# A streaming batch-norm: loads and stores on two DMA rings with hand-placed semaphores, and the last tile handled as two halves of its rows

## The chip, the cores and the metric

The kernel runs on one core of one Trainium2 chip. Times are device microseconds (us); "before" and "after" are medians of several executions on the same chip. All runs quoted here are of the state "fast" (no run was set aside), with a granted clock of 1.0. A profile shows one execution of each kernel; its span is about 1.8 us shorter than the time of that execution.

## The reference

An inference batch-norm over a tensor of 32 x 256 x 128 x 128 float32 values. For each channel there is one scale and one shift:

```python
def reference(x, gamma, beta, running_mean, running_var):
    eps = 1e-5
    # the four vectors of 256 channels are reshaped to (1, 256, 1, 1)
    return gamma * (x - mean) / np.sqrt(var + eps) + beta
```

It reads 536.9 MB and writes as much; there is one multiply-add per element. The kernel sees `x` as 64 tiles of 128 channels (partitions) by 16384 columns, 8 MB each, so that one partition's row of a tile is 64 KB.

## The kernel before

Three buffers, one DMA ring (a queue of transfers; every load and store of a tile is issued by SyncE, SP in the profile), in groups of three tiles: three loads, then three stores, then the next three loads.

```python
NBUF = 3
GROUPS = [3] * 20 + [2, 2]
AHEAD = 0
# ... parameters: scale_t, shift_t, one column per half of the channels ...

    def load(i):
        t = data.tile([P, HW], f32, tag="t")          # P = 128, HW = 16384
        nc.sync.dma_start(out=t[:], in_=xr[i])
        tiles[i] = t

    def compute(i):
        t = tiles[i]
        cb = i % NCB
        nc.vector.tensor_scalar(out=t[:], in0=t[:],
            scalar1=scale_t[:, cb : cb + 1], scalar2=shift_t[:, cb : cb + 1],
            op0=mybir.AluOpType.mult, op1=mybir.AluOpType.add)

    def store(i):
        t = tiles.pop(i)
        nc.sync.dma_start(out=outr[i], in_=t[:])

    first = 0
    for g, size in enumerate(GROUPS):
        idxs = range(first, first + size)
        for i in idxs:
            compute(i)
        for i in idxs:
            store(i)
        first += size
        # ... load the tiles of the next group ...
```

## Time and profile before

| | |
|---|---|
| time, median | 2486.68 us (2486.56 to 2487.64, 3 runs) |
| DMA engines busy | 99.9% of the span |
| VectorE (DVE) busy | 566.0 us, 23% |
| 64 KB packets | 16384, minimum and median 2.418 us |

First the page of the kernel before: busy time of VectorE; the mean GB/s in 40 equal slices of the span; and the one DMA queue that carries the tiles, with its packets, its MB and the share of 16 engines' span that the packets took.

```profile
DVE 566.0 (23%) x75; ACT 1.6 (0%) x2; POOL 0.2 (0%) x4
GB/s 421 423 439 439 425 436 439 431 431 439 431 431 439 435 426 436 436 431 435 435 435 427 439 434 427 439 434 427 439 437 432 432 437 433 431 437 433 431 437 396
q1 hardware_dynamic: 18432, 1073.75, 99.9%
```

The DMA engines are the bound, from the first slice to the last. The trace's packet records give the unit: one 64 KB row, loaded or stored, takes one DMA engine 2.418 us. Each of 16 engines has 1024 of them, 2476.0 us. The span is 2483.6 us, so only 7.6 us are anything else.

Then the groups of instructions: the 64 passes of VectorE. The columns after the count are busy us, mean ns of one, and idle us before them with what ended most of it.

```profile
L93 DVE TENSOR_SCALAR t<-t,scale_t,shift_t 128x16384 f32<-128x16384 f32 x64 | 564.0, 8812 | 1863.9 <-DMA t<-in_x_dram 1863.8
```

A pass takes 8.81 us, and VectorE idles 1863.9 us waiting for loads. That idle time costs nothing here: the DMA engines are busy for 99.9% of the span meanwhile.

Last, the end of the run in the timeline: start, duration, engine, instruction, and in brackets the idle time before it.

```profile
2424.58 8.81 DVE L93 TENSOR_SCALAR t<-t,scale_t,shift_t 128x16384 f32<-128x16384 f32 x1 [49.09 <-DMA t<-in_x_dram]
2433.42 19.69 SPq L104 DMA_DIRECT2D out_dram<-t  x2
2443.92 8.81 DVE L93 TENSOR_SCALAR t<-t,scale_t,shift_t 128x16384 f32<-128x16384 f32 x1 [10.53 <-DMA t<-in_x_dram]
```

Tile 62 lands at 2424.58 and tile 63 at 2443.92, each starting its pass at once. While the last pass runs to 2452.7, the store of tile 62, issued at 2433.42, has the engines. The last store follows it. The engines are not left without work anywhere in this tail, as windows of 10 us show: length, busy us of each engine with its count of instructions, TensorE's clock, the DMA engines' busy share, and GB/s. (A packet is counted by its start, so that the share of a full window lies somewhat under or over 1.)

```profile
2443.60:2453.60 10.00, 8.81 (x1) 0.00 (x0) 0.00 (x0) 1.00 0.98 426
2453.60:2463.60 10.00, 0.00 (x0) 0.00 (x0) 0.00 (x0) 1.00 1.07 465
2463.60:2473.60 10.00, 0.00 (x0) 0.00 (x0) 0.00 (x0) 1.00 0.97 419
```

A store is about 19.3 us of work for all engines (8 packets of 2.418 us each).

### The profile page before, as it was taken

How to read it: one execution, taken by the hardware profiler on the slowest of the kernel's cores; microseconds unless marked ns; L12 is line 12 of the kernel's file. 1: busy time of each engine (PE TensorE's matmuls, PEld its weight loads, DVE VectorE, ACT ScalarE, POOL GpSimd, SP SyncE). 2: the span in 40 equal slices, each digit the busy share in tenths (PEclk: the TensorE clock that was granted, in tenths of full speed). 3: DMA queues.
4: the chain of work that ended last, by engine and by line, in shares of the span. 5: the costliest groups of instructions: out<-in, count | busy, mean ns of one | idle time of the engine just before them, and what ended most of it. 6: DMA issues, size and time to landing. Idle time of an engine off the chain costs nothing.

```text
span 2483.6 us, 383 instructions
## 1 busy us (share of the span) xinstructions
DVE 566.0 (23%) x75; ACT 1.6 (0%) x2; POOL 0.2 (0%) x4
## 2 busy tenths in 40 slices
DVE  3140404121221213140403121221213040403112
ACT  0000000000000000000000000000000000000000
POOL 0000000000000000000000000000000000000000
DMA  9999999999999999999999999999999999999999
GB/s 421 423 439 439 425 436 439 431 431 439 431 431 439 435 426 436 436 431 435 435 435 427 439 434 427 439 434 427 439 437 432 432 437 433 431 437 433 431 437 396
DMA packets 18442, 1073.77 MB, mean 432 GB/s; under 512 B 2052, under 2 KB 2056, under 8 KB 2056
## 3 DMA queue, kind: packets, MB, share of 16 engines
q1 hardware_dynamic: 18432, 1073.75, 99.9%
q14 instruction: 2, 0.02, 0.0%
q10 hardware_dynamic: 8, 0.00, 0.0%
HBM read 536.88 MB, written 536.87 MB: 432 GB/s over the span
## 4 chain that ended last, share of the span: by engine, by line
another core or an unknown queue 72%; DVE 22%; DMA 4%; issue 0%; DVEq 0%; SPq 0%
DVE t L93 22%; DMA t<-in_x_dram 4%; DVEq L93 0%; SPq L51 0%; SPq L104 0%
## 5 line engine op out<-in xcount | busy, mean ns | idle before, releaser
L93 DVE TENSOR_SCALAR t<-t,scale_t,shift_t 128x16384 f32<-128x16384 f32 x64 | 564.0, 8812 | 1863.9 <-DMA t<-in_x_dram 1863.8
L66 DVE STREAM_TRANSPOSE turned<-rows 32x256 f32<-32x256 f32 x1 | 0.4, 432 | 21.5 <-DMA rows<-in_running_mean_dram 21.5
L78 ACT ACT_TABLE_LOAD x1 | 1.3, 1283 | 2.6 <-issue 2.6
L71 DVE COPY par<-turned 32x8 f32<-32x8 f32 x4 | 0.6, 161 | 0.1
L56 DVE MEMSET rows<- 32x256 f32 x1 | 0.3, 272 | 0.8 <-PEq L132 0.8
L78 ACT ACTIVATE tmp_t<-par,eps_t 128x2 f32<-128x2 f32 x1 | 0.3, 297 | 20.0 <-DVE par L71 20.0
L85 DVE RECIPROCAL tmp_t<-tmp_t 128x2 f32<-128x2 f32 x1 | 0.2, 165 | 0.4 <-ACT tmp_t L78 0.4
L87 DVE TENSOR_TENSOR tmp_t<-par,scale_t 128x2 f32<-128x2 f32 x1 | 0.2, 161 | 0.0
L88 DVE TENSOR_TENSOR shift_t<-par,tmp_t 128x2 f32<-128x2 f32 x1 | 0.2, 161 | 0.0
L86 DVE TENSOR_TENSOR scale_t<-par,tmp_t 128x2 f32<-128x2 f32 x1 | 0.2, 160 | 0.0
L132 POOL MEMSET const-uint8-127<- 128x1 uint8 x1 | 0.1, 103 | 0.0
L132 POOL MEMSET const-bfloat16-1.0<- 128x1 bf16 x1 | 0.1, 101 | 0.0
L132 POOL MEMSET const-float32-0.0<- 128x1 f32 x1 | 0.1, 98 | 0.2 <-issue 0.2
L132 POOL MEMSET const-float32-1.0<- 128x1 f32 x1 | 0.1, 98 | 0.0
L64 DVE MEMSET eps_t<- 128x1 f32 x1 | 0.1, 59 | 0.0
## 6 DMA issues: line engine op xcount, KB each, us to landing
t<-in_x_dram SPq DMA_DIRECT2D x64, 58.0
out_dram<-t SPq DMA_DIRECT2D x64, 49.1
rows<-in_running_var_dram ACTq DMA_DIRECT2D x1, 1.0 KB
rows<-in_gamma_dram ACTq DMA_DIRECT2D x1, 1.0 KB
rows<-in_beta_dram ACTq DMA_DIRECT2D x1, 1.0 KB
rows<-in_running_mean_dram ACTq DMA_DIRECT2D x1, 1.0 KB
```

The lines of the kernel that those rows point to most:

```text
L56: nc.vector.memset(rows, 0.0)
L64: nc.vector.memset(eps_t, eps)
L66: nc.vector.transpose(out=turned[:], in_=rows[:])
L71: nc.vector.tensor_copy(out=par[q * B : (q + 1) * B], in_=blocks[:, :, q, 0:4])
L78: nc.scalar.activation(out=tmp_t[:], in_=var_t, func=mybir.ActivationFunctionType.Sqrt, bias=eps_t[:], scale=1.0,)
L85: nc.vector.reciprocal(out=tmp_t[:], in_=tmp_t[:])
L86: nc.vector.tensor_mul(out=scale_t[:], in0=gamma_t, in1=tmp_t[:])
L87: nc.vector.tensor_mul(out=tmp_t[:], in0=mean_t, in1=scale_t[:])
L88: nc.vector.tensor_sub(out=shift_t[:], in0=beta_t, in1=tmp_t[:])
L93: nc.vector.tensor_scalar(out=t[:], in0=t[:], scalar1=scale_t[:, cb : cb + 1], scalar2=shift_t[:, cb : cb + 1], op0=mybir.AluOpType.mult, ...
L132: nc = _bacc.Bacc("TRN2", target_bir_lowering=False, num_devices=1)
```

## The change

Its intent: loads on the SP ring and stores on the ring of ScalarE (ACT), so that neither waits behind the other; semaphores (counters on which one engine waits for another) placed by hand instead of by the scheduler; and the last tile cut into partitions 0 to 63 and 64 to 127, so that the first half can be stored while the second is still being loaded or computed. The diff's core (the parameter arithmetic is the same, with waits spelled out):

```diff
 NBUF = 3
-GROUPS = [3] * 20 + [2, 2]
 ...
+        last = NT - 1
+        half = [slice(0, P // 2), slice(P // 2, P)]
+        for i in range(NT):
+            s, turn = i % NBUF, i // NBUF
+            if i < last:
+                inst = nc.sync.dma_start(out=bufs[s][:], in_=xr[i]).then_inc(loaded[s], 16)
+                if turn:
+                    inst._wait_ge(stored[s], 16 * turn)
+            else:
+                for h in range(2):
+                    inst = nc.sync.dma_start(out=bufs[s][half[h]], in_=xr[i][half[h]]).then_inc(halves[h], 16)
+                    if h == 0:
+                        inst._wait_ge(stored[s], 16 * turn)
 ...
+        def compute(i, rows=slice(0, P)):       # as before, on bufs[s][rows]; then_inc(done, 1)
+        def store(i, rows=slice(0, P)):
+            s = i % NBUF
+            return nc.scalar.dma_start(out=outr[i][rows], in_=bufs[s][rows]).then_inc(stored[s], 16)
+
+        for i in range(last):
+            compute(i)._wait_ge(loaded[i % NBUF], 16 * (i // NBUF + 1))
+            store(i)._wait_ge(done, i + 1)
+        for h in range(2):
+            compute(last, half[h])._wait_ge(halves[h], 16)
+            store(last, half[h])._wait_ge(done, last + h + 1)
+        for s in range(NBUF):
+            turns = (NT - s + NBUF - 1) // NBUF
+            nc.sync.wait_ge(stored[s], 16 * (turns + (1 if last % NBUF == s else 0)))
```

More of the change, by code (lines that the diff above doesn't have):

```diff
@@ L9 @@
 NBUF = 3
-GROUPS = [3] * 20 + [2, 2]
-AHEAD = 0
 @with_exitstack
@@ L37 @@
     NQ = P // B
-    assert sum(GROUPS) == NT and max(GROUPS) <= NBUF
-    params = ctx.enter_context(tc.tile_pool(name="params", bufs=1))
-    data = ctx.enter_context(tc.tile_pool(name="data", bufs=NBUF))
     xr = x.rearrange("n (cb p) h w -> (n cb) p (h w)", p=P)
     outr = out.rearrange("n (cb p) h w -> (n cb) p (h w)", p=P)
-    ctx.enter_context(tc.manual_schedule())
-    tiles = {}
-    def load(i):
-        t = data.tile([P, HW], f32, tag="t")
-        nc.sync.dma_start(out=t[:], in_=xr[i])
-        tiles[i] = t
@@ L55 @@
-    rows = params.tile([B, C], f32, tag="rows")
-    nc.vector.memset(rows, 0.0)
-    for r, ap in enumerate((running_var, gamma, beta, running_mean)):
-        nc.scalar.dma_start(out=rows[r : r + 1, :], in_=ap.rearrange("(o c) -> o c", o=1))
-    for i in range(AHEAD + GROUPS[0]):
-        load(i)
-    eps_t = params.tile([P, 1], f32, tag="eps")
-    nc.vector.memset(eps_t, eps)
-    turned = params.tile([B, C], f32, tag="turned")
-    nc.vector.transpose(out=turned[:], in_=rows[:])
-    par = params.tile([P, NCB, 4], f32, tag="par")
@@ L69 @@
-    blocks = turned.rearrange("p (cb q r) -> p cb q r", cb=NCB, q=NQ)
-    for q in range(NQ):
-        nc.vector.tensor_copy(out=par[q * B : (q + 1) * B], in_=blocks[:, :, q, 0:4])
-    var_t, gamma_t, beta_t, mean_t = (par[:, :, r] for r in range(4))
-    scale_t = params.tile([P, NCB], f32, tag="scale")
-    shift_t = params.tile([P, NCB], f32, tag="shift")
-    tmp_t = params.tile([P, NCB], f32, tag="tmp")
-    nc.scalar.activation(
-        out=tmp_t[:],
-        in_=var_t,
-        func=mybir.ActivationFunctionType.Sqrt,
-        bias=eps_t[:],
-        scale=1.0,
-    )
@@ L85 @@
-    nc.vector.reciprocal(out=tmp_t[:], in_=tmp_t[:])
-    nc.vector.tensor_mul(out=scale_t[:], in0=gamma_t, in1=tmp_t[:])
-    nc.vector.tensor_mul(out=tmp_t[:], in0=mean_t, in1=scale_t[:])
-    nc.vector.tensor_sub(out=shift_t[:], in0=beta_t, in1=tmp_t[:])
-    def compute(i):
-        t = tiles[i]
-        cb = i % NCB
-        nc.vector.tensor_scalar(
-            out=t[:],
-            in0=t[:],
-            scalar1=scale_t[:, cb : cb + 1],
-            scalar2=shift_t[:, cb : cb + 1],
-            op0=mybir.AluOpType.mult,
-            op1=mybir.AluOpType.add,
-        )
@@ L102, in store @@
-    def store(i):
-        t = tiles.pop(i)
-        nc.sync.dma_start(out=outr[i], in_=t[:])
-    first = 0
-    for g, size in enumerate(GROUPS):
-        idxs = range(first, first + size)
-        for i in idxs:
-            compute(i)
-        for i in idxs:
-            store(i)
-        first += size
-        more = GROUPS[g + 1] if g + 1 < len(GROUPS) else 0
-        for i in range(first + AHEAD, min(first + AHEAD + more, NT)):
-            load(i)
+    params = ctx.enter_context(tc.tile_pool(name="params", bufs=1))
@@ new lines @@
+    data = ctx.enter_context(tc.tile_pool(name="data", bufs=1))
+    bufs = [data.tile([P, HW], f32, name=f"t{s}", tag=f"t{s}") for s in range(NBUF)]
+    rows = params.tile([B, C], f32, name="rows", tag="rows")
+    turned = params.tile([B, C], f32, name="turned", tag="turned")
+    par = params.tile([P, NCB, 4], f32, name="par", tag="par")
+    eps_t = params.tile([P, 1], f32, name="eps_t", tag="eps")
+    std_t = params.tile([P, NCB], f32, name="std_t", tag="std")
+    rstd_t = params.tile([P, NCB], f32, name="rstd_t", tag="rstd")
@@ new lines @@
+    scale_t = params.tile([P, NCB], f32, name="scale_t", tag="scale")
+    ms_t = params.tile([P, NCB], f32, name="ms_t", tag="ms")
+    shift_t = params.tile([P, NCB], f32, name="shift_t", tag="shift")
+    loaded = [tc.alloc_semaphore(f"loaded{s}") for s in range(NBUF)]
+    stored = [tc.alloc_semaphore(f"stored{s}") for s in range(NBUF)]
+    done = tc.alloc_semaphore("done")
+    fetched = tc.alloc_semaphore("fetched")
+    vec = tc.alloc_semaphore("vec")
+    act = tc.alloc_semaphore("act")
@@ new lines, with step @@
+    halves = [tc.alloc_semaphore(f"half{h}") for h in range(2)]
+    with tc.tile_critical():
+        count = [0]
+        def step(inst, sem=None, value=None):
+            if sem is not None:
+                inst._wait_ge(sem, value)
+            elif count[0]:
+                inst._wait_ge(vec, count[0])
+            inst.then_inc(vec, 1)
+            count[0] += 1
+            return count[0]
+        last = NT - 1
[11 more added lines that the diff above has]
+                        inst._wait_ge(stored[s], 16 * turn)
+        step(nc.vector.memset(eps_t[:], eps))
+        zeroed = step(nc.vector.memset(rows[:], 0.0))
+        for r, ap in enumerate((running_var, gamma, beta, running_mean)):
+            inst = nc.scalar.dma_start(out=rows[r : r + 1, :], in_=ap.rearrange("(o c) -> o c", o=1))
+            if r == 0:
+                inst._wait_ge(vec, zeroed)
+            inst.then_inc(fetched, 16)
+        step(nc.vector.transpose(out=turned[:], in_=rows[:]), fetched, 64)
+        blocks = turned.rearrange("p (cb q r) -> p cb q r", cb=NCB, q=NQ)
+        for q in range(NQ):
+            placed = step(nc.vector.tensor_copy(out=par[q * B : (q + 1) * B], in_=blocks[:, :, q, 0:4]))
+        var_t, gamma_t, beta_t, mean_t = (par[:, :, r] for r in range(4))
+        nc.scalar.activation(
+            out=std_t[:],
+            in_=var_t,
+            func=mybir.ActivationFunctionType.Sqrt,
+            bias=eps_t[:],
+            scale=1.0,
+        )._wait_ge(vec, placed).then_inc(act, 1)
+        step(nc.vector.reciprocal(out=rstd_t[:], in_=std_t[:]), act, 1)
+        step(nc.vector.tensor_mul(out=scale_t[:], in0=gamma_t, in1=rstd_t[:]))
+        step(nc.vector.tensor_mul(out=ms_t[:], in0=mean_t, in1=scale_t[:]))
+        ready = step(nc.vector.tensor_sub(out=shift_t[:], in0=beta_t, in1=ms_t[:]))
+        nc.vector.wait_ge(vec, ready)
+        def compute(i, rows=slice(0, P)):
+            s, cb = i % NBUF, i % NCB
+            return nc.vector.tensor_scalar(
+                out=bufs[s][rows],
+                in0=bufs[s][rows],
+                scalar1=scale_t[rows, cb : cb + 1],
+                scalar2=shift_t[rows, cb : cb + 1],
+                op0=mybir.AluOpType.mult,
+                op1=mybir.AluOpType.add,
+            ).then_inc(done, 1)
+        def store(i, rows=slice(0, P)):
[10 more added lines that the diff above has]
+            nc.sync.wait_ge(stored[s], 16 * (turns + (1 if last % NBUF == s else 0)))
```

## The prediction

> What bounds the kernel. The page's DMA rows show the 16 DMA engines busy 99.9% of the span of 2483.6 us on one queue, moving 1073.77 MB at 432 GB/s. The trace's packet records hold 16384 packets of 64 KB whose minimum and median are both 2.418 us, for loads and stores alike, so 1024 packets per engine need 2476.0 us. VectorE is busy 23%; its 64 passes of 8.81 us hide behind transfers. The timeline of the end shows no bubble: the last load lands at 2443.9, the store of the tile before fills the last pass (to 2452.8), and the last store then takes its 19.4 us. Room for a gain: the 7.6 us between 2476.0 and 2483.6 (0.3%), unless the packet time changes.
>
> What the change does.
> (a) Loads stay on the SP ring, stores move to the ACT ring. [...] four 1 KB parameter loads on the ACT ring landed at 22.6 us, their 8 packets one per 2.42 us, that is in turn with the 64 KB packets of the other ring. With three buffers a cycle is 116 us (period in the chain of waits); a load and a store at half rate each (about 38.7 us) plus a pass of 8.8 us need 86 us, so neither ring runs dry.
> (b) Loads and stores now alternate packet by packet instead of. In the old trace only the packets at a turn from load to store are slow: about 0.1 us per engine at a typical turn, 1.2 us at the first. If every alternation paid this, 512 turns would cost 50 us; I expect 0 to 15 us.
> (c) The last tile is halved by partitions. Passes of half the partitions still take 8.8 us each (16384 columns), hidden. [...] No transfer of 64 partitions is in the trace. If it holds, the last loads (8 packets per engine, at 4.84 instead of 2.42 us) cost up to 19 us more, partly hidden by interleaved stores, and the last two stores 19 us more with nothing to hide them. If it does not hold, halving wins nothing, since the old tail has no bubble. I give the penalty two chances in three.
> (d) Hand-placed semaphores remove waits of the SP queue that are off the bound: under 3 us.
>
> Sum: 2486.7 + about 5 (mixing) + about 17 (halves, weighted; 30 when it applies) - 2 gives about 2506 us. Range 2480 to 2532. Faster by over 2%: 0.03; within 2%: 0.88; slower by over 2%: 0.09.
>
> What would show it. DMA busy near 99%; the 64 KB packets of the steady part still 2.42 us; a store landing every 38.7 us. (c) right: the last 64-partition transfers have packets near 4.8 us, GB/s in the last two slices falls well below 396, and the end comes some 50 us after the last load instead of 40. (c) wrong: those packets stay at 2.42 us and the time is 2482 to 2490.
>
> What would make it wrong: read-write mixing that costs 5% in every packet (slower by more than 2%), or mixing that lets an engine's load and store overlap so that packets of both rings take less than 2.42 us in effect (faster). Either shows in the GB/s row.

(In (c), "it" and "the penalty" mean a supposition, shown by no trace at that time: that a transfer of 64 partitions takes twice the 2.42 us per packet, hence 4.84. Measured since: medians of 4.5 to 5.0 us per packet in the changed kernel and 5.11 us in E6, with 17.8 us of excess for the halved load alone (E5) and 20.2 us for the halved store alone (E6), where (c) has up to 19 and 19. The sum: 2486.7 + 5 + 17 - 2 = 2506.7.)

## The result, and the profile after

2524.93 us median of 4 runs (2520.78 to 2531.57) against 2486.62 us for the kernel before on the same chip: a ratio of 1.0156, 95% interval 1.0133 to 1.0179. So the change costs 38 us, within 2% but clear of noise. Ratios here are the mean time of one kernel's fast runs over that of the other's runs of the same rounds, so not quite the ratio of the medians quoted.

The page after: the GB/s row and the two queues.

```profile
GB/s 415 431 431 433 440 436 432 432 432 432 433 436 438 433 429 432 431 432 433 435 433 425 431 432 432 432 432 432 432 432 432 432 432 432 432 432 432 432 342 256
q1 hardware_dynamic: 9232, 536.88, 50.2%
q10 hardware_dynamic: 9240, 536.88, 49.6%
```

The 38 slices before the last two look like before; the last two fall from 437 and 396 GB/s to 342 and 256. The loads now go through q1 and the stores through q10, half the time each.

The passes by shape:

```profile
L119 DVE TENSOR_SCALAR t<-t,scale_t,shift_t 128x16384 f32<-128x16384 f32 x63 | 555.2, 8813 | 1860.9 <-DMA t<-in_x_dram 1860.7
L119 DVE TENSOR_SCALAR t<-t,scale_t,shift_t 64x16384 f32<-64x16384 f32 x2 | 17.6, 8810 | 35.2 <-DMA t<-in_x_dram 35.2
```

Half the partitions take as long as all of them, 8.81 us; half the columns take 4.55 us (E3 below). So the columns set the time of these passes.

The end in the timeline (the last load's halves are issued from 2421.34 on):

```profile
2421.34 5.48 SPq L86 DMA_DIRECT2D t<-in_x_dram  x2
2432.57 8.81 DVE L119 TENSOR_SCALAR t<-t,scale_t,shift_t 128x16384 f32<-128x16384 f32 x1 [31.54 <-DMA t<-in_x_dram]
2462.11 8.80 DVE L119 TENSOR_SCALAR t<-t,scale_t,shift_t 64x16384 f32<-64x16384 f32 x1 [20.72 <-DMA t<-in_x_dram]
2485.39 8.82 DVE L119 TENSOR_SCALAR t<-t,scale_t,shift_t 64x16384 f32<-64x16384 f32 x1 [14.48 <-DMA t<-in_x_dram]
```

The two halves land at 2462.11 and 2485.39. They follow tile 62's landing (2432.57) by 29.5 and 52.8 us. In the two-ring variant E1 below, which differs only in keeping the last tile whole, the whole tile follows by 38.9 us.

And 10 us windows of the same stretch, with the columns named:

```profile
core 0: us, DVE busy (x) ACT busy (x) POOL busy (x), PEclk, DMA share, GB/s
2434.70:2444.70 10.00, 6.69 (x1) 0.00 (x0) 0.00 (x0) 1.00 1.02 216
2474.70:2484.70 10.00, 0.00 (x0) 0.00 (x0) 0.00 (x0) 1.00 1.00 413
2484.70:2494.70 10.00, 8.82 (x1) 0.00 (x0) 0.00 (x0) 1.00 1.14 288
2494.70:2504.70 10.00, 0.00 (x0) 0.00 (x0) 0.00 (x0) 1.00 1.00 275
```

From 2434.7 to 2444.7 and again from 2494.7, the engines are fully busy (1.02, 1.00) and yet move 216 and 275 GB/s. Between, at 2474.7, with few half-tile packets under way, they move 413. It is not idle time; the packets themselves are longer (median 5.13 us from 2434.7, 2.418 us from 2474.7).

For all kernels the packet records can be added up. "Excess" is the time of the 64 KB packets above 2.418 us, per engine (the sum over 16); "end" means packets that start in the last 110 us. "Idle" is the rest of the stretch from the first packet's start to the last one's end. One profile of each kernel:

| profile of | first start to last end | excess, until the end | excess, end | idle |
|---|---|---|---|---|
| before | 2480.4 | 4.4 | 0.0 | -0.1 |
| after | 2521.1 | 11.5 | 31.3 | 2.2 |

(Neighbouring packets overlap by a few ns each, 4 ns most often in these two profiles, which makes "idle" too small by about 3 us.) The sums agree: 2476.0 + 4.4 + 0.0 - 0.1 = 2480.4, and 2476.0 + 11.5 + 31.3 + 2.2 = 2521.1. Of the 40.7 us between them, 31.3 lie in long packets at the end, 7.1 in slightly longer load packets before it, and 2.3 in idle engines.

### The profile page after: what moved, and what is told of

Same layout as the page of the kernel before. It is cut to its first block, busy times and chain, and to the rows that moved or that the text cites. A ratio compares the mean times of both kernels' runs of the same rounds, so it can differ in the third digit from the quotient of the medians.

```text
span 2524.7 us, 266 instructions
## 1 busy us (share of the span) xinstructions
DVE 574.9 (23%) x76; ACT 1.6 (0%) x2; POOL 0.2 (0%) x4
## 4 chain that ended last, share of the span: by engine, by line
another core or an unknown queue 93%; DMA 4%; DVE 1%; SPq 1%; issue 0%; ACTq 0%; ACT 0%; DVEq 0%
DMA out_dram<-t 2%; DMA t<-in_x_dram 2%; DVE t L119 1%; DMA rows<-in_running_mean_dram 1%; SPq L81 1%; ACTq L94 0%; DVE par L102 0%; DVE turned L98 0%; ACT std_t L104 0%; DVE rows L92 0%; DVE rstd_t L111 0%; DVE shift_t L114 0%; DVE ms_t L113 0%; DVE scale_t L112 0%
## 5 line engine op out<-in xcount | busy, mean ns | idle before, releaser
L119 DVE TENSOR_SCALAR t<-t,scale_t,shift_t 128x16384 f32<-128x16384 f32 (+1 forms) x65 | 572.8, 8813 | 1896.1 <-DMA t<-in_x_dram 1895.9
L98 DVE STREAM_TRANSPOSE turned<-rows 32x256 f32<-32x256 f32 x1 | 0.4, 433 | 21.5 <-DMA rows<-in_running_mean_dram 21.5
```

The costliest lines, as they stand in the source:

```text
L98: step(nc.vector.transpose(out=turned[:], in_=rows[:]), fetched, 64)
L119: return nc.vector.tensor_scalar(out=bufs[s][rows], in0=bufs[s][rows], scalar1=scale_t[rows, cb : cb + 1], scalar2=shift_t[rows, cb : cb + 1],
```

## The experiments

Theory A: the loss is mostly the row halves, because packets of a transfer of partitions 0 to 63 or 64 to 127 take about twice as long (medians of 4.5 to 5.0 us in the profile of the changed kernel, 2.418 us, the median too, for its other packets). Why they do was not shown by any trace or run. Rivals: B, the two rings or the semaphores cost it; C, halving as such costs it (more transfers and waits); D, any transfer of 64 partitions is slow, whichever they are. All results were correct. Eleven kernels were run.

| variant | median us (lowest to highest) | ratio to before, 95% interval |
|---|---|---|
| E1 after, last tile whole | 2504.49 (2482.24 to 2505.69), 6 runs | 1.0056 (1.0032 to 1.0081) |
| E2 before, last tile in row halves | 2528.88 (2527.02 to 2530.82), 4 runs | 1.0169 (1.0156 to 1.0182) |
| E3 after, column halves | 2502.97 (2484.27 to 2504.98), 6 runs | 1.0054 (1.0033 to 1.0076) |
| E4 after, partitions 32-95, 0-31, 96-127 | 2524.24 (2520.79 to 2525.94), 4 runs | 1.0148 (1.0134 to 1.0163) |
| E5 after, only the load in row halves | 2514.76 (2503.44 to 2516.59), 4 runs | 1.0099 (1.0081 to 1.0117) |
| E6 after, only the store in row halves | 2518.81 (2507.85 to 2522.45), 4 runs | 1.0123 (1.0105 to 1.0140) |
| E7 as E6, one half on each ring | 2513.25 (2511.66 to 2517.63), 4 runs | 1.0109 (1.0095 to 1.0123) |
| E8 before, stores on the ACT ring | 2500.74 (2482.09 to 2503.01), 6 runs | 1.0035 (1.0007 to 1.0063) |
| E9 E1 with one load, one store in flight | 2487.60 (2485.43 to 2488.89), 5 runs | 1.0003 (0.9991 to 1.0015) |
| E10 E9 with the first three loads free | 2486.00 (2485.40 to 2487.54), 5 runs | 0.9998 (0.9984 to 1.0012) |
| E11 after, in step as E10 | 2525.48 (2524.09 to 2527.74), 4 runs | 1.0155 (1.0138 to 1.0172) |

The same sums of packets as above, in us per engine:

| profile of | first start to last end | excess, until the end | excess, end | idle |
|---|---|---|---|---|
| E1 | 2500.1 | 10.3 | 0.2 | 13.6 |
| E2 | 2525.6 | 5.1 | 35.6 | 8.8 |
| E3 (a quick run) | 2478.9 | 2.2 | 0.4 | 0.3 |
| E4 | 2518.7 | 9.0 | 19.6 | 14.0 |
| E5 | 2510.8 | 6.9 | 17.8 | 10.0 |
| E6 | 2517.1 | 10.2 | 20.2 | 10.7 |
| E7 | 2506.3 | 4.4 | 13.6 | 12.2 |
| E8 | 2497.3 | 7.7 | 0.2 | 13.5 |
| E9 | 2482.4 | 5.1 | 0.1 | 1.2 |
| E10 | 2480.7 | 5.3 | 0.1 | -0.7 |
| E11 | 2522.4 | 8.2 | 36.5 | 1.7 |

### E1: the changed kernel with a whole last tile

```diff
             else:
-                for h in range(2):
-                    inst = nc.sync.dma_start(out=bufs[s][half[h]], in_=xr[i][half[h]]).then_inc(halves[h], 16)
-                    if h == 0:
-                        inst._wait_ge(stored[s], 16 * turn)
+                inst = nc.sync.dma_start(out=bufs[s][:], in_=xr[i]).then_inc(halves[0], 16)
+                inst._wait_ge(stored[s], 16 * turn)
 ...
-        for h in range(2):
-            compute(last, half[h])._wait_ge(halves[h], 16)
-            store(last, half[h])._wait_ge(done, last + h + 1)
+        compute(last)._wait_ge(halves[0], 16)
+        store(last)._wait_ge(done, last + 1)
 ... the final wait counts one store less
```

> The changed kernel with the last tile loaded, computed and stored whole; rings and semaphores stay. Theory A (the loss is mostly the row halves[...]): the 31 us of packet excess found in the tail of the changed kernel's trace go, about 2493 us, 0.2 to 0.5% slower than the kernel before, last packets at 2.42 us. Rival B (two rings mixing reads and writes, or the hand-placed semaphores, cost the time): stays near 2525 us.

The long packets at the end are gone (excess 31.3 to 0.2), but the time was neither theory's 2493 nor 2525. The six runs are 2502.5 to 2505.7 five times, and 2482.24 once. The profiled run was one of the slow kind. Its end, in the timeline and then in windows (columns as above):

```profile
2429.74 8.81 DVE L117 TENSOR_SCALAR t<-t,scale_t,shift_t 128x16384 f32<-128x16384 f32 x1 [29.83 <-DMA t<-in_x_dram]
2468.61 8.81 DVE L117 TENSOR_SCALAR t<-t,scale_t,shift_t 128x16384 f32<-128x16384 f32 x1 [30.07 <-DMA t<-in_x_dram]
```

```profile
2453.60:2463.60 10.00, 0.00 (x0) 0.00 (x0) 0.00 (x0) 1.00 1.01 439
2463.60:2473.60 10.00, 4.99 (x1) 0.00 (x0) 0.00 (x0) 1.00 0.12 52
2473.60:2483.60 10.00, 3.83 (x1) 0.00 (x0) 0.00 (x0) 1.00 0.75 321
2483.60:2493.60 10.00, 0.00 (x0) 0.00 (x0) 0.00 (x0) 1.00 0.97 419
```

Here is a bubble that the kernel before did not have. From 2463.6 to 2473.6 the engines are 12% busy, 2 of 16 on average. The last tile lands at 2468.61, its pass takes 8.81 us, and only then is its store issued; the earlier stores are used up by then on all engines but one. The packet records show how late that one is. These are the starts (us from the span's start) of the last ten load packets, and of the last packets of the store before the last:

```
E1  loads   2446.4 2446.4 2446.5 2447.0 2449.5 2451.1 2451.3 2456.1 2458.6 2463.4
E1  stores  ... 2463.6 2464.0 2464.1 2465.6 2465.8 2468.2 2470.6 2473.1 2475.5 2477.9
```

118 of the 128 packets of the last load had started by 2446.3; the last one started 17 us later. The stores at the end of the second row come 2.4 us apart, beginning where that load packet ends (2463.4 + 2.4): one engine, working through packets that the others have long done. So a DMA engine lags 12 to 17 us behind the rest by these starts, the load counts as landed only when that engine has done its share, and the others wait through that and the pass. The semaphores say it directly. A load's semaphore goes up in 16 steps, read here as one for each engine, and the trace keeps the time of each: for the last load fifteen come between 2449.7 and 2456.3, the sixteenth at 2468.6. Nor is the lag a matter of the end alone. From the first to the last step of a load it is 0.4 us at 23 us, 8.4 at 481 us, 18.3 at 955 us, and 18.6 to 21.5 for every whole tile from 1200 us on. Such a bubble is what halving might fill (but see E3 and E11). (The expectations below call the lag "drift".)

### E2: the kernel before with a halved last tile

```diff
+    def pieces(i):
+        return [slice(0, P)] if i < NT - 1 else [slice(0, P // 2), slice(P // 2, P)]
     def load(i):
         t = data.tile([P, HW], f32, tag="t")
-        nc.sync.dma_start(out=t[:], in_=xr[i])
+        for r in pieces(i):
+            nc.sync.dma_start(out=t[r], in_=xr[i][r])
```

(and the same `for r in pieces(i)` around the pass and the store.)

> The kernel before (one ring, groups of three) with only the last tile's load, pass and store halved by rows. A: with nothing interleaved to hide them, 8 load packets and 8 store packets per engine at 4.84 instead of 2.42 us, +38 us, about 2525 us. B: about 2487 us, as the kernel before.

2528.88 us, +42: theory A held, and B fell for the larger part. The windows of its end, while the halves are loaded:

```profile
2438.60:2448.60 10.00, 4.13 (x1) 0.00 (x0) 0.00 (x0) 1.00 1.01 210
2448.60:2458.60 10.00, 4.47 (x1) 0.00 (x0) 0.00 (x0) 1.00 1.01 210
```

All engines busy (1.01), 210 GB/s, on one ring, with the scheduler's semaphores: by these figures 32 packets in 10 us, about 5.05 us each, where 4.84 was expected. The excess at the end is 35.6 us. Another 8.8 us are idle, mostly in the last 20 us, where the busy share of the same windows falls to 0.53 and 0.11.

### E3: halves of columns

```diff
-        half = [slice(0, P // 2), slice(P // 2, P)]
+        half = [slice(0, HW // 2), slice(HW // 2, HW)]
 ...
-                    inst = nc.sync.dma_start(out=bufs[s][half[h]], in_=xr[i][half[h]]).then_inc(halves[h], 16)
+                    inst = nc.sync.dma_start(out=bufs[s][:, half[h]], in_=xr[i][:, half[h]]).then_inc(halves[h], 16)
```

(and `[:, cols]` in the pass and the store.)

> The changed kernel with the last tile halved by columns: 128 partitions by 8192, packets of 32 KB. A [...]: packets of 1.21 us, the same time as the whole-tile variant within 2 us, about 2493 us. Rival C (halving itself costs: twice the transfers, semaphores and waits at the end): stays well above the whole-tile variant, up to 2525 us.

As often, transfers, semaphores and passes as in the changed kernel, but 128 partitions each: 2502.97 us, level with E1's 2504.49, with packets of 32 KB at 1.213 us and no excess at the end (0.4). Rival C falls. The passes also are halved:

```profile
L119 DVE TENSOR_SCALAR t<-t,scale_t,shift_t 128x8192 f32<-128x8192 f32 x2 | 9.1, 4546 | 44.0 <-DMA t<-in_x_dram 44.0
```

4.55 us where a row half took 8.81. Yet five of the six runs are as slow as E1's (2502.5 to 2505.0). So halving by columns won 1.5 us on E1's median, no more; no slow run of E3 was profiled, so its tail is not known. The profiled run is the quick one (2484.27) and has no bubble (idle 0.3), nearly no slow load packets (excess 2.2 before the end, E1 10.3), and no lag: from the first to the last step of a load's semaphore it is 2.4 to 3.0 us for every whole tile after 200 us.

### E4: which 64 partitions

```diff
-        half = [slice(0, P // 2), slice(P // 2, P)]
+        half = [slice(32, 96), slice(0, 32), slice(96, P)]
 ...
-        for h in range(2):
-            compute(last, half[h])._wait_ge(halves[h], 16)
-            store(last, half[h])._wait_ge(done, last + h + 1)
+        for h in range(len(half)):
+            nc.vector.wait_ge(halves[h], 16)
+        compute(last)
+        for h in range(len(half)):
+            store(last, half[h])._wait_ge(done, last + 1)
 ... three semaphores and three loads in place of two
```

> The changed kernel with the last tile's load and store cut into partitions 32 to 95, 0 to 31 and 96 to 127, one whole pass between. [...] Excess half of that of row halves: 10 to 19 us over the whole-tile variant, about 2503 to 2512 us. Rival D (any transfer of 64 partitions or fewer runs slow, since each engine gets half the rows): the middle packets are near 4.84 us too and the time is about 2525 us or more.

(Theory A expected packets of 2.42 us for the middle partitions and about 4.84 us for the two quarters.)

The clearest reading is in the last store, where nothing else runs. The first window holds 48 of the middle partitions' 64 packets and already 16 of the quarters' (hence the 1.23); the second holds the quarters alone:

```profile
2492.50:2502.50 10.00, 0.00 (x0) 0.00 (x0) 0.00 (x0) 1.00 1.23 419
2502.50:2512.50 10.00, 0.00 (x0) 0.00 (x0) 0.00 (x0) 1.00 0.97 210
```

419 GB/s, then 210. By packets, in order of their start: the first 64 of the store (partitions 32 to 95) have a median of 2.427 us, the last 64 (0 to 31 and 96 to 127) 5.051 us. For the load it is 2.418 and 4.522 us. So it is not the number of partitions: rival D falls, and the set of partitions decides: 2.427 us for 32 to 95, and 5.11 us for 0 to 63 (E6 below). The trace gives these rates; it does not show what makes them. The excess at the end, 19.6 us, is 63% of the changed kernel's 31.3, and of the store alone half of E6's (10.4 against 20.2 us). The time, 2524.24, was above the 2503 to 2512 expected, because that was counted from the 2493 expected of the whole tile. Over E1 as it was measured it is 19.8 us, just over the 10 to 19 foreseen; the bubble is there as in E1 (14.0 us idle, 13.6 in E1).

### E5, E6, E7: load or store, and one half on each ring

E5 keeps the halved load, then one whole pass and one whole store; E6 keeps the halved store. E7 is E6 with the second half of the store issued by the other ring:

```diff
-        for h in range(2):
-            store(last, half[h])._wait_ge(done, last + 1)
+        store(last, half[0])._wait_ge(done, last + 1)
+        s = last % NBUF
+        nc.sync.dma_start(out=outr[last][half[1]], in_=bufs[s][half[1]]).then_inc(stored[s], 16)._wait_ge(done, last + 1)
```

> The changed kernel with only the last tile's load in row halves; one whole pass, one whole store. [...] its load packets take 4 to 5 us (excess up to 19 us per engine), the last store's stay at 2.42 us. Time between the whole-tile variant (2504) and the changed kernel (2525), or up to 2525 if engines also sit idle during the whole pass of 8.8 us.

> The changed kernel with only the last tile's store in row halves; load and pass whole. [...] store packets near 5 us at the end, about 20 us over the whole-tile variant, near 2522. If only writes to SBUF are limited: packets of 2.42 us and 2504 us.

> As the variant with only the store in row halves (2519, store packets near 5 us), but the lower half is stored by the ACT ring and the upper half by the SP ring at the same time. If each engine simply takes turns, [...] packets stay near 5 us and the time near 2519. If the turns of different engines fall apart, [...] packets go towards 2.42 us and the time towards the whole-tile variant's 2504.

(What is cut from E6's first case leaves its condition out: that reads of SBUF are slowed as writes are. What is cut from E7's two cases is the author's ground for them, which was not shown.)

E5: 2514.76, load packets of 4.99 us (median of the first half) and 4.47 (second), excess at the end 17.8. E6: 2518.81, store packets of 5.11 us in both halves, excess 20.2. So the half stores, which read SBUF, are slowed as the half loads, which write it, are. The windows of E6 while both half stores run:

```profile
2480.70:2490.70 10.00, 0.00 (x0) 0.00 (x0) 0.00 (x0) 1.00 1.01 210
2490.70:2500.70 10.00, 0.00 (x0) 0.00 (x0) 0.00 (x0) 1.00 1.01 223
```

E7: 2513.25, excess at the end 13.6 against 20.2. Where only one half's packets were under way they took 5.1 us; where both rings were active, between 2.4 and 5.1. In time E7 and E6 are not told apart: the intervals of their ratios overlap (1.0095 to 1.0123 and 1.0105 to 1.0140). Putting the halves on two rings is at best a partial cure.

### E8: two rings, everything else as before

```diff
-        nc.sync.dma_start(out=outr[i], in_=t[:])
+        nc.scalar.dma_start(out=outr[i], in_=t[:])
```

> The kernel before with one word changed: stores issued on the ACT ring; groups, scheduler's semaphores and whole tiles stay. Theory A2 (two rings let the engines drift apart, so that the last load lands late and engines idle before the last store): like the whole-tile variant, 2495 to 2505 us, often with a quick run near 2483, and some us of idle engines at the end. Rival (hand-placed semaphores cause it): 2487 us.

One word brings E1's behaviour: 2499.97 to 2503.01 in four runs, 2482.09 and 2482.17 in two. The profiled run is of the slow kind, with 13.5 us of idle engines at the end (the last pass starts at 2465.70):

```profile
2450.00:2460.00 10.00, 0.00 (x0) 0.00 (x0) 0.00 (x0) 1.00 0.97 419
2460.00:2470.00 10.00, 4.30 (x1) 0.00 (x0) 0.00 (x0) 1.00 0.17 72
```

So the bubble comes from the two rings, and the hand-placed semaphores neither make nor cure it.

### E9 and E10: keeping the engines in step

E9 is E1 with two more waits: a load is issued when the load before has landed on all engines, a store when the store before has. E10 leaves out the wait for the first three loads.

```diff
+            if turn:
+                nc.sync.wait_ge(stored[s], 16 * turn)
             if i < last:
                 inst = nc.sync.dma_start(out=bufs[s][:], in_=xr[i]).then_inc(loaded[s], 16)
-                if turn:
-                    inst._wait_ge(stored[s], 16 * turn)
+                if i:                                   # E10: if turn:
+                    inst._wait_ge(loaded[(i - 1) % NBUF], 16 * ((i - 1) // NBUF + 1))
 ...
         def store(i, rows=slice(0, P)):
             s = i % NBUF
+            if i:
+                nc.scalar.wait_ge(stored[(i - 1) % NBUF], 16 * ((i - 1) // NBUF + 1))
 ... the last tile's load waits likewise
```

> The whole-tile variant of the changed kernel with two more waits: a load is issued only when the load before it has landed on all engines, a store only when the store before it has. If drift between engines makes the bubble at the end (A2), this brings them together at each tile: all runs near 2482 us, as the one quick run of the whole-tile variant, little idle time at the end, load packets back at 2.42 us. If something else makes it, it stays bimodal near 2504 us; if the rings run empty at each landing, it is over 2504 us.

> The one-in-flight variant (2487.6) without its extra wait on the first three loads, where no store runs beside them: its trace has about 2 us of idle engines in the first 65 us, against 0.3 in the kernel before. 2485 to 2486 us in all runs; at best level with the kernel before, since both are within 0.5% of the 2476 us that 1024 packets of 2.418 us take. If the first three loads start the drift, it is bimodal again, near 2504 in most runs.

Five runs of 2485.43 to 2488.89 (E9) and five of 2485.40 to 2487.54 (E10): one kind of run only. The end of E10, in windows around its last pass:

```profile
2440.00:2450.00 10.00, 4.73 (x1) 0.00 (x0) 0.00 (x0) 1.00 0.98 426
2450.00:2460.00 10.00, 4.08 (x1) 0.00 (x0) 0.00 (x0) 1.00 0.97 419
2460.00:2470.00 10.00, 0.00 (x0) 0.00 (x0) 0.00 (x0) 1.00 0.73 315
```

The bubble has gone from 12% busy to 73% in its worst window. The last ten load packets start within 1.2 us of each other (2438.9 to 2440.1; 17.0 us in E1), and from the first to the last step of a load's semaphore it is 3.7 to 4.7 us for every whole tile after 200 us. The waits hold no engine up for long (1.2 us idle in E9, -0.7 in E10), but keep the lag in E10 at these 3.7 to 4.7 us, where in E1 it grew to 18.6 and more, and the bubble goes with the lag. E10 is level with the kernel before (0.9998, interval 0.9984 to 1.0012); no variant is faster beyond doubt. Single runs of E1 and E8 reached 2482, 0.2% under the kernel before, but nothing here makes them do so.

### E11: row halves, in step

The waits of E10 added to the changed kernel as it is.

> The changed kernel as it is, row halves included, with the waits that keep one load and one store in flight. If the loss is the sum of two separate terms, [...] (31 us of packet excess in the changed kernel) and the drift (about 7 us of slow load packets in the steady part; its bubble of about 11 us is hidden by the halves), this one keeps the first and loses the second: 2486 + 31 = 2517 us, up to 2524 if the halves' loads are hidden less. [...]

(The first term, 31 us, is the excess of the row halves. The last sentence, cut, had 2486 us as the time if they cost so much only because of the lag.)

2525.48 us, as the changed kernel (2524.93) and just over the range that the sum of two terms gave. The excess at the end is 36.5 us, so the row halves cost what they cost without a lag as in E1. The second half of the expectation, that the slow load packets would go, failed: the excess before the end was 8.2 us (changed kernel 11.5, E10 5.3). So the two losses do not add: in step, the halves cost 39 us (E11 against E10, 2486.00); out of step they cost only 20 (after against E1), where most of the bubble's idle time is gone (13.6 to 2.2 us). That the halves fill it with work is argued from this figure, which counts a slow packet as busy; column halves, with no such packets, won only 1.5 us on the median (E3).

## Why the prediction was right or wrong

The step of the prediction that failed is a term of its sum, "about 17 (halves, weighted; 30 when it applies)": the profile of the changed kernel has 31.3 us of long packets in its place. A second step failed too. "So neither ring runs dry" left no term for the tail, while two rings alone cost 18 us (E1 against before), where the sum had 5 - 2. The two do not add: by way of E1 the rings cost 18 us and the halves 20 more, by way of E2 the halves cost 42 and the rings nothing (after 2524.93, E2 2528.88). In the changed kernel's own profile the long packets are 31.3 of the 40.7 us, which is why they are named first.

- What bounds the kernel: right. The engines' 1024 packets of 2.418 us stay the floor in every variant: 2476.0 us, where the shortest stretch of packets in any profile is 2478.9 us (E3).
- (c), the row halves: the slow packets were right, and near the length foretold (near 4.8 us; 5.0 and 4.5 for the load's halves, 4.5 and 5.0 for the store's). What makes them slow was not shown. The size of the term in the sum was the main error. "about 17 (halves, weighted; 30 when it applies)" entered 17 us; the profile has 31.3. With 30 the forecast would have been 2520; with 17 it was 2506, +0.8% where +1.56% was measured. The mean of two cases was a time that neither case predicts. The range, 2480 to 2532, held the result.
- (c), second part, "halving wins nothing, since the old tail has no bubble": nearly right in what it says of halving (column halves won 1.5 us on E1's median), but the reason missed that the tail of two rings has a bubble where the old one has none (E1, 13.6 us idle). So without slow packets the time would not have been "2482 to 2490": column halves gave 2503 in the median.
- (a), "so neither ring runs dry": right for the steady part, as idle engines there amount to 0.3 us, and tiles land 38.7 to 38.9 us apart (2275.91, 2314.80, 2353.46, 2392.22), at the 38.7 us foretold. Wrong at the end, since the estimate took all 16 engines as one and did not allow for one that lags.
- (b), mixing: booked at 5 us, measured 7.1 (excess before the end, 11.5 against 4.4). Right in size, but by luck: E3's quick run mixes loads and stores on two rings as E1 does and has 2.2, less than the kernel before, so mixing alone need not cost it. The slow packets are loads: in the steady part 9.5 us of excess are on the load ring and 0.2 on the store ring.
- (d), semaphores: nothing measurable. SP's queue still waits 2359.9 us before its loads of whole tiles (before: 950.3 us before loads and 1451.7 us before stores). E8, with the scheduler's, behaves as E1, with those placed by hand. The gain of 2 us in the sum was not seen.
- "the end comes some 50 us after the last load instead of 40": wrong. The second half lands at 2485.39 and the span ends at 2524.7, 39.3 us later, as before (2443.92 to 2483.6, 39.7). The first half's store is under way by then.

Still open is what puts one engine behind and starts the slow load packets in some runs and not in others. Both go together in some profiles (E1, E8: 10.3 and 7.7 us of early excess, a late engine; E3's quick run: 2.2 and none). But E7 has a late engine (12.2 us idle) with the early excess of the kernel before, 4.4, and E11, in step, still has 8.2; so neither is shown to cause the other. The profiles do not name the engine of a packet. Quick and slow runs of E1 can't be compared directly either, as its quick run was not profiled.

## What to carry to other kernels

Cut a transfer by columns, keeping all 128 partitions; if it must be by rows, measure the very rows, because 64 rows starting at 32 ran at full rate (2.427 us per packet, E4) and 64 starting at 0 at half (5.11 us, E6). With the DMA engines 99.9% busy as here, a second ring had next to nothing to win (0.2% in single runs) and one engine fell behind (in E1 by 12 to 17 us; 13.5 us idle in E8); judge a cut in the tail by the tail of the new schedule, not the old. And put a cost that either applies or not into a forecast as two cases, not as their mean.
